# A transformer kernel whose weights pass in tiles of 2,048 columns instead of 1,024

## The chip, the core and the metric

The kernel runs on one core of a Trainium2 chip. The metric is the device time of one execution in microseconds. Before the change the median of three runs is 2656.81 us (2655.06 to 2656.96).

The engines that matter: TensorE (PE in the profile; PEld is its weight load) multiplies, VectorE (DVE) and ScalarE (ACT) work on elements, SyncE (SP) issues the loads. One issue is carried out by the core's 16 DMA engines together.

## The reference, cut to what matters

The input is 256 tokens of 1,024 features, in float32. Two blocks follow one another:

```
first block, 2 layers:  x = LN(a*x + hybrid_mixer(x));  x = LN(a*x + f(x))
    f: layer 0 a dense SwiGLU (2816 wide); layer 1 eight experts (3584 wide), 2 per token
second block, 2 layers: x = LN(a*x + swiglu/2); x = LN(a*x + attention(x))
                        x = LN(a*x + memory_attn(x, mem)); x = LN(a*x + swiglu/2)
swiglu(x, w_gate, w_up, w_down) = (silu(x @ w_gate) * (x @ w_up)) @ w_down
memory_attn: k, v = split(mem @ w_kv), 256 memory tokens, 4 heads of 256
```

The attention of layer 0 is a global one and a windowed one side by side ("ab"), that of layer 1 a neighbourhood one ("mc"). `hybrid_mixer` is a gated linear attention beside a spatial gating.

## The kernel before, in words

Nearly all time goes into matmuls against weights that are read once from memory, some 650 MB. Each float32 weight is split on the chip into a rounded part (hi) and a remainder (lo), each activation likewise, and each product is three matmuls (`mm3`: hi by hi, lo by hi, hi by lo, lines 207 to 209), with 512 columns of output.

`split_weight` (line 190) is the path of every weight tile of 128 x 1024: SyncE loads 512 KB into a `raw` tile (line 193), ScalarE casts it to `whi` (line 195), VectorE subtracts to get `wlo` (line 197). The three tiles come from rings of seven, nine and eight (`wraw`, `whi`, `wlo` in `body`), 4 KB per partition each, 96 KB together. A raw slot comes free when the subtraction has read it, a hi or lo slot when the last matmul on it is done; the load, cast or subtraction that needs the slot waits for that. A tile is 2 blocks of 128 rows by 512 columns where 512 outputs are made from all 1,024 features (`accumulate_k4`), or one block of 128 rows by 1,024 columns where 1,024 outputs are made (`accumulate_k2`); `units(c, w, u, n)` makes 2n of them.

The Python code is the order of issue only in outline: a scheduler places every instruction in its engine's queue when the program is built, and each engine then works through its queue in that order. So one long instruction in front of a short one on VectorE delays it, and the engines meet through semaphores.

The stages, in order: hybrid mixer, dense FFN, hybrid mixer, experts, FFN, ab, memory attention, FFN, FFN, mc, memory attention, FFN. In an FFN, five groups of gate and up columns (and one of half the width) and then three groups of down rows are each used by two blocks of 128 tokens. In the expert stage (`moe`) the tokens of one expert are gathered into 128 slots, so each tile is used by one pass: eight gate and up tiles, four down tiles per iteration, seven iterations per expert, 56 in all. Per iteration ScalarE computes silu, VectorE multiplies (line 770), TensorE transposes (line 304), the result is split (hTh, hTl, lines 295 and 296), and `down` of the iteration before runs. An expert's result is split (yh, yl) and scattered back with matmuls (lines 758 and 759) and an addition into X on VectorE (line 760); the gather of the next two experts (line 725) is spread over iterations.

The memory's keys and values do not depend on the tokens. They are eight `MemBlock`s, each with two tiles of memory rows and four of weights, two halves of 48 matmuls. Two are done at the start of the expert stage, one at its end (loaded ahead of the last down tiles, computed after them), three in ab, two in mc, filling gaps there.

Of the kernel before, what the change touches and what calls it, by code (L numbers as in the profile page):

```python
# [8 lines left out]
F32 = mybir.dt.float32  # L9
# [16 lines left out]
UW = 1024  # L26
# [65 lines left out]
def k4_units(w):  # L92
    n = w.shape[-1]
    b = w.reshape(4, 2, P, n // 512, 512).transpose(3, 0, 2, 1, 4)
    return np.ascontiguousarray(b).reshape(-1, P, UW)


def k2_units(w):
    return np.ascontiguousarray(w).reshape(-1, P, UW)

# [15 lines left out]
def layout(a):  # L116
# [5 lines left out]
    o["memT"] = feature_major(a["mem_2"].reshape(S, D))  # L122
# [20 lines left out]
    moe = np.empty((8, 7, 12, P, UW), np.float32)  # L143
    for i, n in enumerate(("exp_w_gate", "exp_w_up")):
        w = a[n][0].reshape(8, 4, 2, P, 7, 512).transpose(0, 4, 1, 3, 2, 5)
        moe[:, :, 4 * i:4 * i + 4] = w.reshape(8, 7, 4, P, UW)
    moe[:, :, 8:12] = a["exp_w_down"][0].reshape(8, 7, 4, P, UW)
    o["moe"] = moe.reshape(8 * 84, P, UW)
# [41 lines left out]
def split_weight(c, src):  # L190
    nc = c.nc
    raw = c.wraw.tile([P, UW], F32, name="raw")
    nc.sync.dma_start(raw, src)
    hi = c.whi.tile([P, UW], F32R, name="whi")
    nc.scalar.copy(hi, raw)  # L195
    lo = c.wlo.tile([P, UW], F32R, name="wlo")
    nc.vector.tensor_sub(lo, raw, hi.bitcast(F32))  # L197
    return hi, lo


def units(c, dram, u0, n):
    return [split_weight(c, dram[2 * u0 + i]) for i in range(2 * n)]
# [9 lines left out]
def accumulate_k4(c, ps, xk, us):  # L212
    for k in range(8):
        h, l = us[k // 2]
        sl = slice(512 * (k % 2), 512 * (k % 2) + 512)
        mm3(c, ps, *xk(k), h[:, sl], l[:, sl], k == 0, k == 7)


def accumulate_k2(c, pss, xk, us, k0, nk, half_major=False):
    order = [(i, half) for i in range(len(us)) for half in range(2)]  # L220
    if half_major:
        order.sort(key=lambda o: o[1])
    for i, half in order:
        h, l = us[i]
        k = k0 + i
        sl = slice(512 * half, 512 * half + 512)
        mm3(c, pss[half], *xk(k), h[:, sl], l[:, sl], k == 0, k == nk - 1)
# [19 lines left out]
class MemBlock:  # L247
# [3 lines left out]
    def load(self):  # L251
        c = self.c
        self.m = [split_weight(c, c.A["memT"][i]) for i in range(2)]
        self.us = units(c, c.A[f"m_kv{self.l}"], 4 * self.which + 2 * self.blk, 2)

    def at(self, k, sl):
        o = 256 * (k % 4)
        return [x[:, o + sl.start:o + sl.stop] for x in self.m[k // 4]]

    def half(self, half):  # L260
        c, nc = self.c, self.c.nc
        ps = c.acc.tile([P, 512], F32, name="acc")
        if self.which == 0:
            for f in (2 * half, 2 * half + 1):
                out = ps[:, 256 * (f % 2):256 * (f % 2) + 256]
                for k in range(8):
                    wh, wl = self.us[k // 2]
                    sl = slice(512 * (k % 2) + P * f, 512 * (k % 2) + P * f + P)
# [13 lines left out]
    def steps(self):  # L282
        def first():
            self.load()
            self.half(0)

        return [first, lambda: self.half(1)]
# [100 lines left out]
def project(c, w, u0, nblk, xT, epi, us=None):  # L388
    us = us or units(c, w, u0, 2 * nblk)
    for t in range(2):  # L390
        pss = []
        for b in range(nblk):
            ps = acc_tile(c)
            accumulate_k4(c, ps, tok(xT, t), us[4 * b:4 * b + 4])
            pss.append(ps)
        epi(t, pss)
# [16 lines left out]
def ffn(c, w, X, xT, ln_idx, halved, want_xT=True):  # L413
    nc = c.nc
    with c.tc.tile_pool(name="ffn", bufs=1) as fp:
# [3 lines left out]
        for j in range(6):  # L419
            us = units(c, w, 4 * j, 4 if j < 5 else 2)  # L420
            n = 512 if j < 5 else 256
            for t in range(2):
                g = acc_tile(c)
                accumulate_k4(c, g, tok(xT, t), us[:4])
# [3 lines left out]
                if j < 5:  # L428
                    u = acc_tile(c)
                    accumulate_k4(c, u, tok(xT, t), us[4:])  # L430
                else:
                    u = g[:, 256:]
# [8 lines left out]
        for u0, n in ((0, 3), (3, 4), (7, 4)):  # L441
            us = units(c, w, 22 + u0, n)
            for t in range(2):
                accumulate_k2(c, pss[t], tok((hh, hl), t), us, 2 * u0, 22, u0 == 7)
# [3 lines left out]
                if u0 == 7:  # L448
# [328 lines left out]
def moe(c, X, xT, ln_idx):  # L777
    nc, A = c.nc, c.A
    W = A["moe"]
    with c.tc.tile_pool(name="moeb", bufs=1) as c.big, c.tc.tile_pool(name="moe", bufs=1) as mp:  # L780
# [11 lines left out]
        def gu(e, j):  # L792
# [3 lines left out]
            for b in range(2):  # L796
                accumulate_k4(c, pss[b], slots_of(xg, e % 2), us[4 * b:4 * b + 4])
# [56 lines left out]
def crowded(c, mp, W, slot, gate, XS, Xn):  # L854
    nc, tc = c.nc, c.tc
    for e in range(N_EXP):
# [6 lines left out]
        with tc.For_i(0, 7, 1) as j:  # L863
            def halves(u):
                raw = c.lnp.tile([P, D], F32, name="lnb")
                nc.sync.dma_start(raw, W[bass.ds(j * 12 + (84 * e + u), 1), :, :].rearrange("a p n -> (a p) n"))
                for half in range(2):
                    sl = slice(512 * half, 512 * half + 512)
                    hi = mp.tile([P, 512], F32R, name="chi")
                    nc.scalar.copy(hi, raw[:, sl])  # L870
                    lo = mp.tile([P, 512], F32R, name="clo")
                    nc.vector.tensor_sub(lo, raw[:, sl], hi.bitcast(F32))
                    yield half, hi, lo

            pss = [acc_tile(c), acc_tile(c)]
            for b in range(2):
                for i in range(4):
                    for half, hi, lo in halves(4 * b + i):
                        k = 2 * i + half
# [3 lines left out]
            for k in range(4):  # L883
                for half, hi, lo in halves(8 + k):
# [128 lines left out]
def mixer_ab(c, X, xT, ln_idx):  # L1013
    nc, A = c.nc, c.A
    with c.tc.tile_pool(name="ab", bufs=1) as ap:
# [89 lines left out]
        for b in take(c, c.F[3]):  # L1105
            steps += b.steps()
# [4 lines left out]
def mixer_c(c, X, xT, ln_idx):  # L1111
    nc, A = c.nc, c.A
    with c.tc.tile_pool(name="mc", bufs=1) as ap:
# [58 lines left out]
        for b in take(c, c.F[4]):  # L1172
            steps += b.steps()
# [54 lines left out]
def body(tc, A, out, stages=STAGES):  # L1228
# [4 lines left out]
    with tc.tile_pool(name="const", bufs=1) as cp, \  # L1233
            tc.tile_pool(name="wraw", bufs=7) as c.wraw, tc.tile_pool(name="whi", bufs=9) as c.whi, \
            tc.tile_pool(name="wlo", bufs=8) as c.wlo, \
# [7 lines left out]
        c.early = []  # L1243
        for i in range(4):
            raw = c.wraw.tile([P, UW], F32, name="raw")
            nc.sync.dma_start(raw[:, 0:512], A["xT"][i // 2][:, 512 * (i % 2):512 * (i % 2) + 512])
            ks = slice(2 * i, 2 * i + 2)
            split(c, raw[:, 0:512].rearrange("p (k t s) -> p k t s", k=2, t=2), xT[0][:, ks], xT[1][:, ks])
            if stages[0].startswith("hyb"):
                c.early.append(split_weight(c, A[f"h_in{stages[0][3]}"][i]))  # L1250
# [42 lines left out]
```

## Time and profile before

| what | value |
|---|---|
| median of three runs | 2656.81 us |
| the profiled execution | 2656.44 us, its span 2654.6 us, mean granted clock 0.996 |
| TensorE busy | 2596.9 us, 98% of the span |
| VectorE busy | 1899.9 us, 72%; of this 1407.2 in 1193 subtractions (line 197) |
| ScalarE busy | 1483.8 us, 56%; of this 1194.0 in 1193 casts (line 195) |
| moved by DMA | 658.65 MB, mean 248 GB/s, 69.7% of the 16 engines' time |
| loads of expert weights | 672 of 512 KB |

The page's shares are means over twelve stages that differ: the expert stage takes from about 400 to 1490 us and moves over half of the bytes; FFN stages use each tile twice. A matmul's busy time overlaps its neighbours', so distances from start to start tell the pace. A row of the timeline gives start, duration, engine, line and operation, output and inputs, and in brackets the idle time before it with what ended it. Rows with xN are N such instructions in a run.

### The profile page before, as it was taken

What the parts mean: (1) busy time and instruction counts of PE and PEld (TensorE: products, weight loads), DVE (VectorE), ACT (ScalarE), POOL (GpSimd) and SP (SyncE); (2) the same over time, 40 slices, a digit from 0 to 9 for tenths busy, and PEclk for the clock granted to TensorE, in tenths of its full rate; (3) what the DMA queues carried; (4) which work ended last, traced back from release to release, by engine and by line L of the source; (5) the groups of instructions that cost most, each with busy time, mean ns of one, the idle gap of its engine ahead of it and who ended that gap; (6) DMA issues with size and microseconds to landing.
All of it is one profiled execution on the core that took longest, in us unless ns stands there. A gap on an engine that the chain in (4) does not pass through costs nothing. (4 is left out here: it accounts for less than half of the span.)

```text
span 2654.6 us, 34354 instructions
## 1 busy us (share of the span) xinstructions
PE 2596.9 (98%) x12226; PEld 2110.3 (79%) x12226; DVE 1899.9 (72%) x2306; ACT 1483.8 (56%) x1780; POOL 46.8 (2%) x57
## 2 busy tenths in 40 slices
PE   8999999999999999999999999999999999999998
PEld 6888778877777777787777788788888888788887
DVE  6754668888888888888888655866755656566664
ACT  5444447676777777767777444554443443544552
POOL 1000000000000000000000000100000000000000
PEclk9999999999999999999999999999999999999999
DMA  7555536999999999999999655544554655744562
GB/s 287 175 180 192 199 127 249 341 355 348 333 348 354 341 338 347 345 347 332 358 346 355 221 191 206 184 168 175 206 187 149 221 204 154 231 155 175 206 206 88
DMA packets 193980, 658.65 MB, mean 248 GB/s; under 512 B 33094, under 2 KB 33288, under 8 KB 193288
## 3 DMA queue, kind: packets, MB, share of 16 engines
q1 hardware_dynamic: 193800, 656.37, 69.7%
q8 instruction: 98, 1.61, 0.2%
q14 instruction: 82, 0.67, 0.1%
HBM read 651.05 MB, written 5.24 MB: 247 GB/s over the span
## 5 line engine op out<-in xcount | busy, mean ns | idle before, releaser
L197 DVE TENSOR_TENSOR wlo<-raw,whi 128x1024 fp32r<-128x1024 f32 x1193 | 1407.2, 1219 | 237.1 <-ACT whi L195 113.2
L195 ACT CAST whi<-raw 128x1024 fp32r<-128x1024 f32 x1193 | 1194.0, 1053 | 373.2 <-PE acc L209 291.0
L207 PE MATMUL acc<-whi,xh 128*128 128x512 f32 x1312 | 522.0, 398 | 6.6 <-ACT whi L195 6.3
L209 PE MATMUL acc<-whi,xl 128*128 128x512 f32 x1312 | 514.9, 393 | 0.0
L208 PE MATMUL acc<-wlo,xh 128*128 128x512 f32 x1312 | 514.1, 392 | 0.0
L208 PE MATMUL acc<-wlo,xgh 128*128 128x512 f32 x896 | 356.9, 398 | 5.3 <-DVE wlo L197 5.3
L207 PE MATMUL acc<-whi,xgh 128*128 128x512 f32 x896 | 350.2, 391 | 1.9 <-ACT whi L195 1.9
L209 PE MATMUL acc<-whi,xgl 128*128 128x512 f32 x896 | 350.3, 391 | 0.0
L207 PEld LDWEIGHTS acc<-whi,xh 128*128 128x128 f32 x1312 | 247.5, 189 | 56.5 <-ACT whi L195 6.3
L209 PEld LDWEIGHTS acc<-whi,xl 128*128 128x128 f32 x1312 | 247.0, 188 | 52.0 <-issue 0.5
L208 PEld LDWEIGHTS acc<-wlo,xh 128*128 128x128 f32 x1312 | 247.5, 189 | 50.1 <-DVE wlo L197 0.8
L208 PEld LDWEIGHTS acc<-wlo,xgh 128*128 128x128 f32 x896 | 168.0, 188 | 63.5 <-DVE wlo L197 27.8
L207 PEld LDWEIGHTS acc<-whi,xgh 128*128 128x128 f32 x896 | 168.2, 188 | 40.9 <-ACT whi L195 4.8
L209 PEld LDWEIGHTS acc<-whi,xgl 128*128 128x128 f32 x896 | 168.3, 188 | 32.6
L208 PE MATMUL tp<-wlo,hTh 128*128 128x512 f32 x448 | 180.1, 402 | 7.3 <-DVE wlo L197 7.1
L209 PE MATMUL tp<-whi,hTl 128*128 128x512 f32 x448 | 178.5, 398 | 0.0
L207 PE MATMUL acc<-whi,hh 128*128 128x512 f32 x440 | 172.5, 392 | 0.0
L209 PE MATMUL acc<-whi,hl 128*128 128x512 f32 x440 | 171.4, 390 | 0.0
L208 PE MATMUL acc<-wlo,hh 128*128 128x512 f32 x440 | 171.3, 389 | 0.0
L207 PE MATMUL tp<-whi,hTh 128*128 128x512 f32 x448 | 153.9, 394 | 5.0 <-ACT whi L195 5.0
L296 DVE TENSOR_TENSOR hl<-tp,hh 128x512 fp32r<-128x512 f32 (+1 forms) x60 | 38.8, 647 | 136.9 <-ACT hh L295 135.5
L295 ACT CAST xh<-tp 128x512 fp32r<-128x512 f32 x52 | 30.2, 588 | 172.9 <-PE tp L304 159.2
(254 smaller groups left out, 2490.2 us busy)
## 6 DMA issues: line engine op xcount, KB each, us to landing
raw<-moe_dram SPq DMA_DIRECT2D x672, 512.0 KB, 5.4
raw<-f_dram SPq DMA_DIRECT2D x330, 512.0 KB, 5.0
raw<-h_in_dram SPq DMA_DIRECT2D x40, 512.0 KB, 6.0
raw<-m_kv_dram SPq DMA_DIRECT2D x32, 512.0 KB, 4.5
raw<-c_in_dram SPq DMA_DIRECT2D x24, 512.0 KB, 5.3
raw<-h_out_dram SPq DMA_DIRECT2D x16, 512.0 KB, 4.4
raw<-memT_dram SPq DMA_DIRECT2D x16, 512.0 KB, 4.6
raw<-m_q_dram SPq DMA_DIRECT2D x16, 512.0 KB, 5.6
```

Source lines behind the costliest of these rows:

```text
L195: nc.scalar.copy(hi, raw)
L197: nc.vector.tensor_sub(lo, raw, hi.bitcast(F32))
L207: mm(ps, xh, wh, start=start, stop=False)
L208: mm(ps, xh, wl, start=False, stop=False)
L209: mm(ps, xl, wh, start=False, stop=stop)
L295: c.nc.scalar.copy(dh, ps)
L296: c.nc.vector.tensor_sub(dl, ps, dh.bitcast(F32))
```

## The change

A weight tile gets 2,048 columns: one load of 1 MB, one cast, one subtraction. The rings become four, four and four tiles of 8 KB per partition, again 96 KB. A k4 tile now holds four blocks of rows by 512 columns, a k2 tile two blocks by 1,024. `units` makes n tiles where it made 2n. The three groups of an FFN's down rows become four, four and three tiles (8, 8, 6 blocks of rows) where they were 6, 8 and 8 blocks, so the last group is shorter. The memory rows become one tile of 1 MB, and in ab and mc a block takes over the rows of the block ahead of it instead of loading them again (`block_steps`): 5 loads of 1 MB in place of 16 of 512 KB in all. The first mixer's first two tiles are loaded, cast and subtracted in halves, and the input's transposed copy shares one raw tile. The matmuls are the same and as many, and stand in nearly the same order. (`crowded`, which the inputs do not reach, is adapted alike; its part of the diff is left out, as is the host's reshaping.)

```diff
-UW = 1024
+UW = 2048
...
-def split_weight(c, src):
+def split_weight(c, src, parts=1):
     nc = c.nc
+    n = src.shape[-1]
     raw = c.wraw.tile([P, UW], F32, name="raw")
-    nc.sync.dma_start(raw, src)
     hi = c.whi.tile([P, UW], F32R, name="whi")
-    nc.scalar.copy(hi, raw)
     lo = c.wlo.tile([P, UW], F32R, name="wlo")
-    nc.vector.tensor_sub(lo, raw, hi.bitcast(F32))
+    for i in range(parts):
+        sl = slice(n // parts * i, n // parts * (i + 1))
+        nc.sync.dma_start(raw[:, sl], src[:, sl])
+        nc.scalar.copy(hi[:, sl], raw[:, sl])
+        nc.vector.tensor_sub(lo[:, sl], raw[:, sl], hi[:, sl].bitcast(F32))
     return hi, lo
 
 
 def units(c, dram, u0, n):
-    return [split_weight(c, dram[2 * u0 + i]) for i in range(2 * n)]
+    return [split_weight(c, dram[u0 + i]) for i in range(n)]
...
-    def load(self):
+    def load(self, m=None):
         c = self.c
-        self.m = [split_weight(c, c.A["memT"][i]) for i in range(2)]
+        self.m = m or split_weight(c, c.A["memT"])
...
+def block_steps(blocks):
+    def step(i, half):
+        if half == 0:
+            blocks[i].load(blocks[i - 1].m if i else None)
+        blocks[i].half(half)
+
+    return [lambda i=i, half=half: step(i, half) for i in range(len(blocks)) for half in range(2)]
...
-        for u0, n in ((0, 3), (3, 4), (7, 4)):
+        for u0, n in ((0, 4), (4, 4), (8, 3)):
...
-            tc.tile_pool(name="wraw", bufs=7) as c.wraw, tc.tile_pool(name="whi", bufs=9) as c.whi, \
-            tc.tile_pool(name="wlo", bufs=8) as c.wlo, \
+            tc.tile_pool(name="wraw", bufs=4) as c.wraw, tc.tile_pool(name="whi", bufs=4) as c.whi, \
+            tc.tile_pool(name="wlo", bufs=4) as c.wlo, \
...
+        raw = c.wraw.tile([P, UW], F32, name="raw")
         for i in range(4):
-            raw = c.wraw.tile([P, UW], F32, name="raw")
-            nc.sync.dma_start(raw[:, 0:512], A["xT"][i // 2][:, 512 * (i % 2):512 * (i % 2) + 512])
+            sl = slice(512 * i, 512 * i + 512)
+            nc.sync.dma_start(raw[:, sl], A["xT"][i // 2][:, 512 * (i % 2):512 * (i % 2) + 512])
...
-                c.early.append(split_weight(c, A[f"h_in{stages[0][3]}"][i]))
+            if i % 2 == 0 and stages[0].startswith("hyb"):
+                c.early.append(split_weight(c, A[f"h_in{stages[0][3]}"][i // 2], 2))
```

VectorE's queue in an iteration of the expert loop with a scatter, before (wlo is a weight's remainder; silu the multiply of line 770; X the scatter's addition; hTl the remainder of the transposed product):

```order
L197 TENSOR_TENSOR wlo<-raw,whi 128x1024 x10
L770 TENSOR_TENSOR silu<-silu,acc 128x512
L197 TENSOR_TENSOR wlo<-raw,whi 128x1024
L760 SCALAR_TENSOR_TENSOR X<-tp,gate,X 128x512
L296 TENSOR_TENSOR hTl<-tp,hTh 128x512
L197 TENSOR_TENSOR wlo<-raw,whi 128x1024 x11
```

The same place after the change:

```order
L776 TENSOR_TENSOR silu<-silu,acc 128x512
L201 TENSOR_TENSOR wlo<-raw,whi 128x2048
L302 TENSOR_TENSOR hTl<-tp,hTh 128x512
L766 SCALAR_TENSOR_TENSOR X<-tp,gate,X 128x512
L201 TENSOR_TENSOR wlo<-raw,whi 128x2048 x5
L776 TENSOR_TENSOR silu<-silu,acc 128x512
```

Six instructions stand in an iteration where twelve stood, and X and hTl have changed places. Behind the multiply comes the second of two down tiles, where before it was the second of four.

VectorE's queue between the first FFN and the second mixer, before, from the second token block's residual sum (line 343) to the layer norm's last step (line 359):

```order
L344 BN_STATS lst<-X 128x6
L197 TENSOR_TENSOR wlo<-raw,whi 128x1024
L353 BN_AGGR lmv<-lst 128x2
L197 TENSOR_TENSOR wlo<-raw,whi 128x1024
L327 TENSOR_SCALAR lrs<-lmv 128x1
L358 SCALAR_TENSOR_TENSOR X<-X,lmv,lng 128x512 x2
L359 SCALAR_TENSOR_TENSOR X<-X,lrs,lnb 128x512 x2
```

The same place after the change:

```order
L350 BN_STATS lst<-X 128x6
L201 TENSOR_TENSOR wlo<-raw,whi 128x2048
L359 BN_AGGR lmv<-lst 128x2
L201 TENSOR_TENSOR wlo<-raw,whi 128x2048
L333 TENSOR_SCALAR lrs<-lmv 128x1
L364 SCALAR_TENSOR_TENSOR X<-X,lmv,lng 128x512 x2
L365 SCALAR_TENSOR_TENSOR X<-X,lrs,lnb 128x512 x2
```

Two subtractions stand inside the layer norm in both; each has twice the columns after the change.

SyncE's queue of loads at the end of the expert stage, before (moe are the experts' tiles, memT and m_kv those of the extra memory block, f_00 the next FFN's):

```order
L193 DMA raw<-moe_dram 128x1024 x657
L193 DMA raw<-memT_dram 128x1024 x2
L193 DMA raw<-m_kv_dram 128x1024 x4
L193 DMA raw<-moe_dram 128x1024 x4
L193 DMA raw<-f_00_dram 128x1024 x7
```

The same place after the change:

```order
L199 DMA raw<-moe_dram 128x2048 x329
L199 DMA raw<-memT_dram 128x2048
L199 DMA raw<-m_kv_dram 128x2048 x2
L199 DMA raw<-moe_dram 128x2048 x2
L199 DMA raw<-f_00_dram 128x2048 x4
```

The memory block's tiles still go ahead of the last down tiles; they are three where they were six, in a ring of four where the rings had seven to nine.

## Rows read from the trace of the kernel before

**Rows 1.** The page: busy time, share of the span, instructions.

```profile
PE 2596.9 (98%) x12226; PEld 2110.3 (79%) x12226; DVE 1899.9 (72%) x2306; ACT 1483.8 (56%) x1780; POOL 46.8 (2%) x57
```

**Rows 2.** Windows (FFN, expert loop, two experts): length, busy by engine, clock, DMA share, GB/s.

```profile
1526.00:1592.40 66.40, 66.40 (x306) 54.95 (x305) 35.64 (x36) 30.57 (x36) 0.00 (x0) 1.00 0.55 191
455.00:1450.00 995.00, 975.30 (x4336) 775.75 (x4335) 857.85 (x825) 708.16 (x795) 0.00 (x0) 1.00 0.95 347
1100.00:1356.50 256.50, 250.84 (x1118) 199.46 (x1117) 221.15 (x212) 182.55 (x206) 0.00 (x0) 1.00 0.95 344
```

**Rows 3.** Groups by line and shape: count, busy us, mean ns, idle before.

```profile
L197 DVE TENSOR_TENSOR wlo<-raw,whi 128x1024 fp32r<-128x1024 f32 x1193 | 1407.2, 1219 | 237.1 <-ACT whi L195 113.2 <-PE acc L208 85.6 <-PE acc L209 9.9
L195 ACT CAST whi<-raw 128x1024 fp32r<-128x1024 f32 x1193 | 1194.0, 1053 | 373.2 <-PE acc L209 291.0 <-DMA raw<-moe_dram 30.1 <-PE acc L208 7.0
...
L296 DVE TENSOR_TENSOR hTl<-tp,hTh 128x512 fp32r<-128x512 f32 x56 | 38.2, 682 | 0.0
...
L295 ACT CAST hTh<-tp 128x512 fp32r<-128x512 f32 x56 | 32.9, 587 | 104.1 <-PE tp L304 104.0
```

**Rows 4.** Timeline, expert loop: TensorE, then VectorE; start, us, instruction, idle before.

```profile
735.87 0.62 PE L207 MATMUL tp<-whi,hTh 128*128 128x512 f32 x2
...
737.01 0.60 PE L304 MATMUL tp<-cst,silu 128*128 128x128 f32 x4
...
737.91 0.40 PE L209 MATMUL tp<-whi,hTl 128*128 128x512 f32 x1
...
739.53 0.61 PE L207 MATMUL tp<-whi,hTh 128*128 128x512 f32 x2
740.64 0.50 PE L208 MATMUL tp<-wlo,hTh 128*128 128x512 f32 x1 [0.50 <-DVE wlo L197]
...
736.07 0.69 DVE L770 TENSOR_TENSOR silu<-silu,acc 128x512 f32<-128x512 f32 x1 [0.66 <-PE acc L209]
736.67 1.22 DVE L197 TENSOR_TENSOR wlo<-raw,whi 128x1024 fp32r<-128x1024 f32 x1
738.11 0.75 DVE L760 SCALAR_TENSOR_TENSOR X<-tp,gate,X 128x512 f32<-128x512 f32 x1 [0.22 <-PE tp L759]
738.78 0.68 DVE L296 TENSOR_TENSOR hTl<-tp,hTh 128x512 fp32r<-128x512 f32 x1
739.37 3.49 DVE L197 TENSOR_TENSOR wlo<-raw,whi 128x1024 fp32r<-128x1024 f32 x3
```

**Rows 5.** Timeline, TensorE, two other iterations of the loop.

```profile
707.61 0.50 PE L208 MATMUL acc<-wlo,xgh 128*128 128x512 f32 x1 [0.76 <-DVE wlo L197]
...
718.28 0.66 PE L304 MATMUL tp<-cst,silu 128*128 128x128 f32 x4 [0.78 <-DVE silu L770]
```

**Rows 6.** Waits in the expert loop: us in total, times, longest.

```profile
ACT whi L195 <- DMA raw<-moe_dram: 28.2, 36, 1.8
...
PE tp L208 <- DVE wlo L197: 6.6, 13, 0.5
```

**Rows 7.** Waits of the load queue, 600 to 1300 us.

```profile
SPq L193 <- DVE wlo L197: 506.4, 452, 2.9
```

**Rows 8.** DMA: 512 KB expert loads (page); two 1 MB loads (tile kT).

```profile
raw<-moe_dram SPq DMA_DIRECT2D x672, 512.0 KB, 5.4
...
DMA to landing us min/median/max: 7.7/7.8/7.8
```

**Rows 9.** Timeline, TensorE: start and end of the expert stage.

```profile
408.74 0.39 PE L209 MATMUL acc<-whi,wlo 128*128 128x256 f32 x1 [0.50 <-DVE wlo L197]
...
1457.93 0.80 PE L207 MATMUL tp<-whi,hTh 128*128 128x512 f32 x1 [4.99 <-ACT whi L195]
```

**Rows 10.** Timeline, first FFN to second mixer: VectorE, then TensorE.

```profile
301.07 1.21 DVE L197 TENSOR_TENSOR wlo<-raw,whi 128x1024 fp32r<-128x1024 f32 x1
...
302.31 1.17 DVE L197 TENSOR_TENSOR wlo<-raw,whi 128x1024 fp32r<-128x1024 f32 x1
...
307.63 0.63 PE L304 MATMUL tp<-cst,X 128*128 128x128 f32 x4 [3.15 <-DVE X L359]
```

More of the change, by code (lines that the diff above doesn't have):

```diff
@@ L213, in accumulate_k4 @@
     for k in range(8):
-        h, l = us[k // 2]
-        sl = slice(512 * (k % 2), 512 * (k % 2) + 512)
+        h, l = us[k // 4]
+        sl = slice(512 * (k % 4), 512 * (k % 4) + 512)
         mm3(c, ps, *xk(k), h[:, sl], l[:, sl], k == 0, k == 7)
 def accumulate_k2(c, pss, xk, us, k0, nk, half_major=False):
-    order = [(i, half) for i in range(len(us)) for half in range(2)]
+    order = [(i, half) for i in range(2 * len(us)) for half in range(2)]
     if half_major:
@@ L223, in accumulate_k2 @@
     for i, half in order:
-        h, l = us[i]
+        h, l = us[i // 2]
         k = k0 + i
-        sl = slice(512 * half, 512 * half + 512)
+        o = D * (i % 2) + 512 * half
+        sl = slice(o, o + 512)
         mm3(c, pss[half], *xk(k), h[:, sl], l[:, sl], k == 0, k == nk - 1)
@@ L447, in ffn @@
                 late = []
-                if u0 == 7:
+                if u0 == 8:
                     xn, st = residual(c, X[t], pss[t], ALPHA * (2.0 if halved else 1.0))
@@ L863, in crowded, with quarters @@
         with tc.For_i(0, 7, 1) as j:
[L864 to L873, printed above, removed]
+            def quarters(u):
+                for i in range(2):
+                    raw = c.lnp.tile([P, D], F32, name="lnb")
+                    src = W[bass.ds(j * 6 + (42 * e + u), 1), :, :].rearrange("a p n -> (a p) n")
+                    nc.sync.dma_start(raw, src[:, D * i:D * i + D])
+                    for half in range(2):
+                        sl = slice(512 * half, 512 * half + 512)
+                        hi = mp.tile([P, 512], F32R, name="chi")
+                        nc.scalar.copy(hi, raw[:, sl])
+                        lo = mp.tile([P, 512], F32R, name="clo")
+                        nc.vector.tensor_sub(lo, raw[:, sl], hi.bitcast(F32))
+                        yield i, half, hi, lo
             pss = [acc_tile(c), acc_tile(c)]
             for b in range(2):
-                for i in range(4):
-                    for half, hi, lo in halves(4 * b + i):
-                        k = 2 * i + half
+                for u in range(2):
+                    for i, half, hi, lo in quarters(2 * b + u):
+                        k = 4 * u + 2 * i + half
                         mm3(c, pss[b], *slots_of(xg, 0)(k), hi, lo, k == 0, k == 7)
@@ L882, in crowded @@
             pss = [acc_tile(c), acc_tile(c)]
-            for k in range(4):
-                for half, hi, lo in halves(8 + k):
+            for u in range(2):
+                for i, half, hi, lo in quarters(4 + u):
+                    k = 2 * u + i
                     mm3(c, pss[half], hT[0][:, k], hT[1][:, k], hi, lo, k == 0, k == 3)
@@ L1104, in mixer_ab @@
         steps = late_steps(c, xT, A["ab_in"], 4, lambda t, ps: q_epi(t, ps, 1))
-        for b in take(c, c.F[3]):
-            steps += b.steps()
+        steps += block_steps(take(c, c.F[3]))
         attend(pair, 8, {i: [f] for i, f in enumerate(steps)})
@@ L1171, in mixer_c @@
             steps += late_steps(c, xT, W, 6 + 2 * n, lambda t, ps, f=f: f(t, ps, 1))
-        for b in take(c, c.F[4]):
-            steps += b.steps()
+        steps += block_steps(take(c, c.F[4]))
         plan = {0: steps[0:2], 1: steps[2:4], 2: steps[4:5], 3: steps[5:6]}
```

42 lines of the change are left out of this document (18 added, 24 removed).

## The prediction, made before the changed kernel had run

> **What bounds the kernel now.** The page's busy line comes first: TensorE 98% of the span, VectorE 72%, ScalarE 56% [rows 1]. An average like that hides stages, so the windows view is next. In an FFN (1526 to 1592.4 us) TensorE is busy for the whole window, with VectorE at 35.6 of 66.4 us and the DMA engines at a share of 0.55 [rows 2]; there is nothing to win there, only something to lose. In the expert loop (455 to 1450 us) TensorE is busy 975.3 of 995 us, VectorE 858, and the DMA share is 0.95 at 347 GB/s [rows 2]. So the loop, a third of the time, is where weights are late: 19.7 us of listed idle. A listed stall of 0.50 us costs more than it shows, since the pipeline restarts: two matmuls start at 739.53 and 739.76, the next would start at 739.99 and starts at 740.64, and its successor another 0.11 us late, 0.76 us in all [rows 4]. By that ratio (1.5) the loop's idle is worth about 30 us, and that is the most that the change can win there.
>
> Who is late? In the waits view the load queue is held by VectorE's subtraction 452 times, 506 us over 700 us [rows 7]: the loads run as fast as raw slots come free. ScalarE waits for data in only 36 cases, 28 us, and TensorE for a lo part in 13 cases, 6.6 us [rows 6]. So the loop is limited by the order of VectorE's queue more than by the transfers, but the transfers are not far behind.
>
> **Term 1: FFN stages, 0.** A tile of 2,048 columns feeds 12 matmuls per token block. A gate/up group is four tiles, all of the ring, read by both token blocks. A slot comes free in the second pass after its 12 matmuls, and three more tiles' work (36 matmuls at 0.23 us, 8.3 us) covers its successor. That needs a cast and a subtraction. Their durations at 2,048 columns are estimates from the shapes at hand [rows 3]: the subtraction takes 682 ns for 512 columns and 1,219 for 1,024, so 537 more per 512 and 2.29 us at 2,048 (two old ones take 2.44); the cast goes 587, 1,053, so about 1.98 us (two old ones 2.11). Together 4.3 us, with 4 us left for the silu, the multiply and the splits that stand in the two queues. Cover gone, an FFN group would lose what exceeds 8.3 us; I see none. From both sides: 0 to +3 us over five FFNs.
>
> **Term 2: the expert loop, -8.8 us.** Per iteration it uses 12 tiles before, 6 after. The timeline shows the stall that repeats [rows 4]. VectorE's queue is multiply (736.07), lo of the second down tile (736.67), the scatter's addition X (738.11), hTl (738.78), and only then lo of the third down tile (739.37), which TensorE wants at 739.99. After the change one down tile holds what two held, and VectorE's order is multiply, lo of the last down tile, hTl, X, next gate tile. The last down tile is thus prepared ahead of X and hTl. In steps: 736.07 + 0.60 (multiply) = 736.67; a step of 2.21 (the three subtractions from 739.37 take 3.49, so a step at 1,024 is 1.135 and at 2,048 about 1.135 + 2 x 0.537 = 2.21) gives 738.88; hTl 0.59 and X 0.67 give 740.14; another 2.21 gives 742.35 for the next gate tile's lo. TensorE gets there at 735.87 + 24 x 0.231 (seven steps from 737.91 to 739.53 in 1.62 us) + 0.90 (transposes and the scatter's first pair, 737.01 to 737.91) = 742.31. So it loses about 0.1 plus the restart's 0.11, 0.2 in place of 0.76: 0.55 us won. The waits view has 13 of these [rows 6]; a window of two experts shows four, and a few records are missing, so I count 16: 8.8 us.
>
> The other two kinds stay. Where the results of an expert are split (0.76 us at 707.61), the two half splits still alternate with subtractions; where TensorE's transposes follow directly on the up pass (0.78 us at 718.28) they wait for the multiply, which does not change [rows 5]. Bounds: all 30 us won; or the coarse ring costs up to the first rival's +28.
>
> **Term 3: start and end of the expert stage, +4.5 us.** At the start the ring of four holds the router's tile, the memory rows and two weight tiles, so the second memory block cannot start loading until the first has been used; before, seven raw and nine hi slots let it in. Today's small stall there is 0.50 us listed [rows 9]. I take one more cast and subtraction at 1,024 columns (1.05 + 1.22) and one such stall with its restart (0.76), +3 us; bounds 0 and +6. At the end, TensorE waits 4.99 us for the hi part of the last down tiles [rows 9], while the extra memory block sits in the ring. It then holds three of four slots, and the two last down tiles go one after the other through the fourth: the second's cast and subtraction (4.3 us) are bare, where before they lay beside matmuls, but the first one's casts are fewer. I take +1.5 us, bounds 0 and +4.3.
>
> **Term 4: from one stage to the next, +2.7 us.** At the first FFN's end the mixer needs both token blocks. VectorE has two subtractions of 1,024 columns inside the second layer norm (301.07 and 302.31), and TensorE waits 3.15 us for X until 307.63 [rows 10]. The order after keeps two there, of 2,048: 2 x (2.29 - 1.22) = +2.1 us. Elsewhere the first token block's pass hides such delays; for the mixers' chains and the attention I add +1 (bounds -1 and +5: each weight instruction in front of a chain step is a microsecond longer, but there are half as many). Shared memory rows remove three 1 MB loads with their casts and subtractions, but in stages where VectorE and ScalarE have room: -0.4 (bounds -2 and 0).
>
> **Sum.** -8.8 + 0 + 4.5 + 2.7 = -1.6. The profiled execution took 2656.44 us (span 2654.6), so 2654.8; the median of the runs is 0.4 above it. I forecast 2655 us: a small gain in the loop that the stage edges nearly eat.
>
> **Rivals.** *The ring of four becomes the limit (slower).* A raw slot's round is the load, cast and subtraction. A single 1 MB load today lands 7.8 us after issue, among other traffic [rows 8]; with 1.98 + 2.29 that is 12.1 us for four tiles, 18.1 us per iteration of six. The iteration today takes 256.5/14 = 18.3 [rows 2]. So the ring decides as soon as a load takes over 7.9 us from issue to landing. One microsecond over that adds 1.5 us to each iteration, 84 us over 56; a third of that, an average landing of 8.2 us, gives +28: 2683 us. For it: the DMA share is 0.95 already, and a slot returns in lumps of 1 MB. Against: with one slot free at a time, a load seldom queues behind a full one, and today's 512 KB land in 5.4 us while queued [rows 8].
>
> *Edges only.* The loop's stall just moves to the next gate tile (my margin there was 0.04 us), and the edges cost their upper half: +6 +4 +2 +3 = 15, so 2671; with the taken values, 2663. For it: every edge in terms 3 and 4 has a bare wait today. Against: the loop's order does move the late subtraction forward.
>
> *The loop fills.* Six fewer loads, casts and subtractions per iteration (VectorE saves 6 x 0.06 = 0.4 us by the steps of term 2, 6 x 0.15 = 0.9 by the means [rows 3]) let VectorE and the transfers run ahead; then 30 us go, less the edges' 7: 2633. For it: VectorE is at 86% in the loop, and stalls come from it. Against: the share of 0.95 leaves 5% of 995 us, and two of the three stalls are order, not load.
>
> The Trainium skill ("DMA: Bandwidth & Descriptors", Rules for kernel authors) asks for at least 1 MiB per DMA for full bandwidth, which would put this change on the side of the third rival. By that rule the loop's 512 KB loads should run below the rate; the trace has the engines at a share of 0.95 with them, several in flight, so it does not bear the rule out here, and the rival's chance rests on VectorE.
>
> **Numbers.** My forecast case, 2644 to 2662, has 0.42; the ring 0.20, edges 0.16, the loop that fills 0.22. A difference under 0.2%, 5.3 us, cannot be told from none here. Of the forecast case 0.17 is faster than 2651.5, 0.21 within, 0.04 slower; of the edges' 0.06 within, 0.10 slower; the ring is slower, the filled loop faster. That makes 0.39 faster, 0.27 the same, 0.34 slower. The range takes in the third rival and the ring's +28: 2632 to 2684.
>
> **What the changed profile would show.** Right: listed stalls before down tiles' lo parts gone, iterations with a scatter near 17.8 us, FFN windows still full, larger single waits at the expert stage's ends and before the second mixer. The ring as the limit: ScalarE's casts waiting for expert loads in most iterations, TensorE waiting for hi. The third rival: TensorE busy over 990 of the loop's 995 us with the loop some 30 us shorter. I am wrong if the FFN windows show gaps, or if a 1 MB expert load takes more than 8 us to land.

## The result, and the profile after

The changed kernel takes 2676.79 us (median of five, 2668.61 to 2677.23) against 2656.06 before: a ratio of 1.0069 (95% interval 1.0054 to 1.0084), 20.7 us slower. I had forecast 2655 and a chance of 0.34 for slower. The profiled execution took 2672.5 us, its span 2670.7, 16.1 over the span before; what the profile can place is thus 16.1 of the 20.7 us.

The page's lines of the changed kernel, as in [rows 1, 3, 8]:

```profile
PE 2594.6 (97%) x12226; PEld 2116.7 (79%) x12226; DVE 1840.3 (69%) x1710; ACT 1416.4 (53%) x1184; POOL 45.8 (2%) x57
...
L201 DVE TENSOR_TENSOR wlo<-raw,whi 128x2048 fp32r<-128x2048 f32 (+1 forms) x597 | 1349.7, 2277 | 452.5 <-ACT whi L200 451.6
L200 ACT CAST whi<-raw 128x2048 fp32r<-128x2048 f32 (+1 forms) x597 | 1126.0, 1903 | 500.9 <-PE acc L213 345.2
...
raw<-moe_dram SPq DMA_DIRECT2D x336, 1024.0 KB, 6.7
```

VectorE and ScalarE are busy 60 and 67 us less, as fewer and longer instructions should make it (2,290 and 1,913 ns a whole tile; the estimates were 2,293 and 1,985). But the subtraction's idle time that ended with the cast went from 113 us [rows 3] to 452: VectorE now often stands still until a cast is done. The windows view, an FFN and the expert loop, as in [rows 2]:

```profile
1534.00:1600.40 66.40, 66.40 (x306) 54.94 (x306) 34.44 (x24) 29.13 (x24) 0.00 (x0) 1.00 0.51 190
455.00:1450.00 995.00, 972.12 (x4360) 785.58 (x4360) 846.62 (x501) 695.10 (x472) 0.00 (x0) 1.00 0.94 349
```

The FFN is full, as before. To see where the time went I cut both traces at ScalarE's silu instructions (124 in either) and took the differences of the stretches between them:

| stretch | before, us | change, us | what the prediction had |
|---|---|---|---|
| first mixer, to the FFN's second silu | 129.40 | +1.8 | in term 4 |
| first FFN | 108.14 | 0.0 | 0 |
| to the second mixer's last silu | 146.87 | +0.8 | +2.1 and part of +1 |
| to the first silu of the experts | 67.13 | +4.7 | in +3 |
| the first two iterations | 26.48 | +3.7 | in +3 |
| the rest of the expert loop | 963.28 | -9.7 | -8.8 |
| its end, to the next FFN's third silu | 76.83 | +6.6 | +1.5 |
| FFN | 96.76 | 0.0 | 0 |
| ab, first memory attention | 274.45 | +5.6 | part of +1, less 0.4 |
| two FFNs | 295.10 | +0.2 | 0 |
| mc, second memory attention | 294.10 | +2.0 | part of +1 |
| last FFN and end | 176.12 | +0.3 | 0 |

So every edge but the one to the second mixer costs more than predicted, 25.8 us in all with the FFNs' remainder, and the loop gives back 9.7.

The loop's iteration with a scatter, TensorE and then VectorE, the changed kernel's answer to [rows 4]:

```profile
752.79 0.39 PE L211 MATMUL acc<-whi,xgh 128*128 128x512 f32 x1
753.02 0.49 PE L212 MATMUL acc<-wlo,xgh 128*128 128x512 f32 x1
753.35 0.40 PE L213 MATMUL acc<-whi,xgl 128*128 128x512 f32 x1
...
746.61 0.69 DVE L776 TENSOR_TENSOR silu<-silu,acc 128x512 f32<-128x512 f32 x1 [0.72 <-PE acc L213]
747.22 2.29 DVE L201 TENSOR_TENSOR wlo<-raw,whi 128x2048 fp32r<-128x2048 f32 x1
749.42 0.69 DVE L302 TENSOR_TENSOR hTl<-tp,hTh 128x512 fp32r<-128x512 f32 x1
750.02 0.74 DVE L766 SCALAR_TENSOR_TENSOR X<-tp,gate,X 128x512 f32<-128x512 f32 x1
750.68 4.48 DVE L201 TENSOR_TENSOR wlo<-raw,whi 128x2048 fp32r<-128x2048 f32 x2
```

The order is the one predicted: multiply, last down tile, hTl, X, next gate tile. From the multiply to the end of the next gate tile's subtraction, the first of the last two, is 746.61 to 752.92 (half of 4.48 us after 750.68), 6.31 us for the 6.28 of term 2, and TensorE has no listed wait: its lo product starts on time at 753.02, the next one 0.10 us late. In the waits view over the loop the waits for a down tile's lo part (`tp`) fell from 13 cases and 6.6 us [rows 6] to 6 and 2.6. But those for a gate or up tile's lo part (`acc`) rose; before, then after:

```profile
PE acc L208 <- DVE wlo L197: 5.3, 7, 0.8
...
PE acc L207 <- ACT whi L195: 1.9, 7, 0.3
```

```profile
ACT whi L200 <- DMA raw<-moe_dram: 105.7, 125, 2.6
...
PE acc L212 <- DVE wlo L201: 12.2, 30, 0.8
...
PE tp L212 <- DVE wlo L201: 2.6, 6, 0.9
```

Of these 30 waits 23 stand at the first lo product of the gate tile behind the down tiles: the stall has in part moved there, as the second rival had it. The iteration shown is one of those without it. To see the sum I added up what each step from one 128x512 matmul to the next takes beyond 0.227 us, over the loop of the table's row: at lo parts of down tiles 14.0 us before and 6.6 after, at lo parts of gate and up tiles 20.7 and 23.7, at hi parts 7.0 and 2.8.

The first line of the second view is the first rival's sign: casts wait for loads 125 times, where it was 36 [rows 6]. But a load lands 6.7 us after issue in the median (at most 8.7 in the loop), under the 7.9 from which the ring would decide, the waits for hi parts are gone from the view, and the loop is shorter. The ring did not take over.

The start and the end of the expert stage on TensorE, as in [rows 9]; the first line is from the kernel before:

```profile
412.20 0.39 PE L209 MATMUL acc<-whi,wlo 128*128 128x256 f32 x1 [1.77 <-DVE wlo L197]
...
411.51 0.50 PE L211 MATMUL acc<-whi 128*128 128x256 f32 x2 [1.09 <-ACT whi L200]
...
416.57 0.58 PE L213 MATMUL acc<-whi,wlo 128*128 128x256 f32 x1 [4.02 <-DVE wlo L201]
...
1460.75 1.22 PE L211 MATMUL tp<-whi,hTh 128*128 128x512 f32 x2 [6.07 <-ACT whi L200]
1463.08 0.80 PE L212 MATMUL tp<-wlo,hTh 128*128 128x512 f32 x1 [1.10 <-DVE wlo L201]
1463.67 0.63 PE L213 MATMUL tp<-whi,hTl 128*128 128x512 f32 x1
1464.10 0.63 PE L212 MATMUL tp<-wlo,hTh 128*128 128x512 f32 x1
...
1469.70 1.22 PE L211 MATMUL tp<-whi,hTh 128*128 128x512 f32 x2 [1.99 <-ACT whi L200]
1472.03 0.80 PE L212 MATMUL tp<-wlo,hTh 128*128 128x512 f32 x1 [1.11 <-DVE wlo L201]
```

At the start waits of 1.09 and 4.02 us stand where 0.50 and 1.77 stood; the second of these, 3.5 us behind the one in [rows 9], I had not seen. At the end the wait for the first down tile is 6.07 us for 4.99, and then come three more, 1.10, 1.99 and 1.11. The matmuls between them start 0.43 us apart (1463.67 to 1464.10): that is TensorE at the lower of its two clock levels (1.2 for 2.4 GHz) after the long wait; the windows view gives a granted clock of 0.50 from 1460 to 1475.

From the first FFN to the second mixer: ScalarE, VectorE, TensorE.

```profile
298.17 5.51 ACT L200 CAST whi<-raw 128x2048 fp32r<-128x2048 f32 x3 [0.79 <-PE acc L213]
...
300.12 2.29 DVE L201 TENSOR_TENSOR wlo<-raw,whi 128x2048 fp32r<-128x2048 f32 x1 [1.56 <-ACT whi L200]
...
302.46 0.50 PE L212 MATMUL acc<-wlo,xh 128*128 128x512 f32 x1 [1.38 <-DVE wlo L201]
...
307.28 0.50 PE L212 MATMUL acc<-wlo,xh 128*128 128x512 f32 x1 [1.78 <-DVE wlo L201]
```

Before, TensorE's one listed wait at this edge was for X [rows 10]. Now it waits twice for the lo part of a tile whose hi part it has begun to use: the cast starts at 298.17, the subtraction only at 300.12 when the whole cast is done, and TensorE goes on at 302.46. These waits lie where TensorE before waited for X, so little is lost by them here: X comes 2.3 us later than before (311.69 for 307.63, less the first mixer's 1.8), term 4 had 2.1, and at the second mixer's last silu 0.8 us are left. In ab a short step is caught behind a cast of 1.89 us; the wait before, then ScalarE and TensorE after:

```profile
1701.41 0.70 PE L955 MATMUL acc<-kT,qT 64*128 64x256 f32 x4 [0.79 <-ACT kT L1077]
...
1710.58 1.89 ACT L200 CAST whi<-raw 128x2048 fp32r<-128x2048 f32 x1
1712.37 0.59 ACT L1086 COPY kT<-tp 128x512 f32<-128x512 f32 x1
...
1713.01 0.70 PE L964 MATMUL acc<-kT,qT 64*128 64x256 f32 x4 [2.31 <-ACT kT L1086]
```

### The profile page after: what moved, and what is told of

Same layout as the page of the kernel before. It is cut to its first block, busy times and chain, and to the rows that moved or that the text cites. A ratio compares the mean times of both kernels' runs of the same rounds, so it can differ in the third digit from the quotient of the medians.

```text
span 2670.7 us, 30301 instructions
## 1 busy us (share of the span) xinstructions
PE 2594.6 (97%) x12226; PEld 2116.7 (79%) x12226; DVE 1840.3 (69%) x1710; ACT 1416.4 (53%) x1184; POOL 45.8 (2%) x57
## 5 line engine op out<-in xcount | busy, mean ns | idle before, releaser
L201 DVE TENSOR_TENSOR wlo<-raw,whi 128x2048 fp32r<-128x2048 f32 (+1 forms) x597 | 1349.7, 2277 | 452.5 <-ACT whi L200 451.6
L200 ACT CAST whi<-raw 128x2048 fp32r<-128x2048 f32 (+1 forms) x597 | 1126.0, 1903 | 500.9 <-PE acc L213 345.2
L211 PE MATMUL tp<-whi,hTh 128*128 128x512 f32 x448 | 166.7, 397 | 8.1 <-ACT whi L200 8.1
L301 ACT CAST xh<-tp 128x512 fp32r<-128x512 f32 x52 | 29.6, 589 | 186.0 <-PE tp L310 167.3
L212 PEld LDWEIGHTS tp<-wlo,hTh 128*128 128x128 f32 x448 | 85.6, 191 | 30.0 <-DVE wlo L201 12.0
```

The lines of the kernel that those rows point to most:

```text
L200: nc.scalar.copy(hi[:, sl], raw[:, sl])
L201: nc.vector.tensor_sub(lo[:, sl], raw[:, sl], hi[:, sl].bitcast(F32))
L211: mm(ps, xh, wh, start=start, stop=False)
L212: mm(ps, xh, wl, start=False, stop=False)
L301: c.nc.scalar.copy(dh, ps)
```

## The experiments

Edits are to the changed kernel unless another is named. The table gives medians of the timed runs, the ratio to the kernel before with its interval, and the stretches of the profiled execution, in us against before (edges: the first mixer, the way to the experts, their first two iterations, ab and mc together). Every stretch is from one execution. The loop of the changed kernel, of that with the extra block behind and of the filler is the same instructions in the same order and came out at -9.7, -5.8 and -7.3, their ab at +5.6, +5.5 and +7.1; so much is scatter.

| kernel | median | ratio | edges | loop | expert end |
|---|---|---|---|---|---|
| changed kernel | 2676.79 | 1.0069 (1.0054-1.0084) | +18.6 | -9.7 | +6.6 |
| extra block behind | 2665.72 | 1.0041 (1.0027-1.0055) | +16.5 | -5.8 | -3.9 |
| cast and subtraction in halves | 2654.64 | 0.9999 (0.9989-1.0008) | +2.2 | -5.3 | +1.9 |
| own slots | 2650.85 | 0.9981 (0.9972-0.9991) | -1.9 | -6.1 | -0.4 |
| 512 KB loads | 2653.94 | 0.9995 (0.9985-1.0004) | -1.7 | -0.9 | -0.6 |
| filler | 2675.59 | 1.0079 (1.0062-1.0096) | +20.2 | -7.3 | +3.3 |
| before, extra block behind | 2651.14 | 0.9983 (0.9973-0.9993) | -0.1 | -0.9 | -4.2 |
| own slots, extra block behind | 2645.78 | 0.9964 (0.9950-0.9978) | -1.3 | -5.8 | -4.9 |
| wide in the loop alone | 2647.71 | 0.9969 (0.9957-0.9982) | +5.2 | -8.2 | -6.4 |
| cast alone in halves | 2682.57 | 1.0102 (1.0085-1.0119) | +17.3 | +3.2 | +5.1 |
| subtraction alone in halves | 2706.61 | 1.0195 (1.0178-1.0212) | +13.1 | +33.9 | +2.4 |
| own slots, block behind, no sharing | 2647.49 | 0.9971 (0.9958-0.9983) | +1.8 | -4.5 | -5.6 |

**The extra memory block behind the last down tiles.**

```diff
         extra = take(c, c.F[2])
-        for b in extra:
-            b.load()
         pe, pj, phT, y = pend
         down(pe, pj, phT, y)
+        for b in extra:
+            b.load()
```

> The changed kernel, with the extra memory block loaded behind the last two down tiles of the expert stage instead of ahead of them. Theory (slots): at the end of the expert stage the block's three tiles hold three of the four slots, so the last down tile's cast waits until TensorE is done with the one before (two waits of 2.4 and 1.5 us, most of it at half clock, where before there is none). With the down tiles first both have a slot: these two waits go, the half-clock stretch is shorter, and the stage's end takes 4 to 7 us less; time 3 to 7 us below the changed kernel. Rival (width): the waits come from the length of one cast and one subtraction, the order of loads does not matter, within 1.5 us of the changed kernel, or later since the block's own tiles come later.

Measured: 11 us below the changed kernel, and the stage's end 10.5 us shorter, of which the loop takes back 3.9; as its instructions are the same, I read nothing into that. The waits for down tiles are gone. The slots theory holds for this place, and its price was larger than I had put it.

**Cast and subtraction in halves.**

```diff
-        nc.scalar.copy(hi[:, sl], raw[:, sl])
-        nc.vector.tensor_sub(lo[:, sl], raw[:, sl], hi[:, sl].bitcast(F32))
+    for i in range(n // 1024):
+        sl = slice(1024 * i, 1024 * (i + 1))
+        nc.scalar.copy(hi[:, sl], raw[:, sl])
+        nc.vector.tensor_sub(lo[:, sl], raw[:, sl], hi[:, sl].bitcast(F32))
```

> The changed kernel (1 MB loads, rings of four slots of 2,048 columns) with each tile cast and subtracted in two halves of 1,024 columns. Theory (width of one instruction): at the stage edges a 2.0 us cast and a 2.3 us subtraction stand in front of short steps and of the first matmul; in halves the edges outside the expert stage's end lose 10 of their 19 us, and the expert loop loses its 10 us gain (the scatter's addition again comes ahead of a down tile's half): 2672 to 2678 in all, edges smaller, loop longer. Rival (slots): the edges keep their cost, loop loses its gain: 2682 to 2690. Rival (loads): as the slots.

Measured: 22 us below the changed kernel, and the same as before the change. The edges fall from +18.6 to +2.2 with loads and slots as they were: the expectation had the direction right and was 17 us too timid, and the rivals of slots and loads fall as the main cause of the edges. By stretch: first mixer +1.8 to +1.6, second mixer +0.8 to -3.6, start of the experts with two iterations +8.4 to +3.5, ab +5.6 to +1.2, mc +2.0 to -0.6. The same place as above, ScalarE, VectorE, TensorE:

```profile
297.96 5.79 ACT L202 CAST whi<-raw 128x1024 fp32r<-128x1024 f32 x6 [0.81 <-PE acc L215]
...
299.05 2.36 DVE L203 TENSOR_TENSOR wlo<-raw,whi 128x1024 fp32r<-128x1024 f32 x2 [0.71 <-ACT whi L202]
...
304.29 0.50 PE L214 MATMUL acc<-wlo,xh 128*128 128x512 f32 x1 [0.70 <-DVE wlo L203]
```

The first subtraction starts 1.09 us after the first cast (1.95 in the changed kernel); of the two waits the first is gone and the second is 0.70 us in place of 1.78, with one of 0.40 behind it.

**Which half of the pair?** The cast alone in halves, then the subtraction alone:

```diff
+    for i in range(n // 1024):          # the cast alone
+        sl = slice(1024 * i, 1024 * (i + 1))
+        nc.scalar.copy(hi[:, sl], raw[:, sl])
+    nc.vector.tensor_sub(lo[:, :n], raw[:, :n], hi[:, :n].bitcast(F32))
...
+    nc.scalar.copy(hi[:, :n], raw[:, :n])          # the subtraction alone
+    for i in range(n // 1024):
+        sl = slice(1024 * i, 1024 * (i + 1))
+        nc.vector.tensor_sub(lo[:, sl], raw[:, sl], hi[:, sl].bitcast(F32))
```

> The changed kernel with the cast in two halves and the subtraction whole. If the wide cast on ScalarE is what costs at the edges (a kT or a silu that waits behind 1.9 us), the edges come near those of the kernel with both in halves, 2657 to 2662. If the wide subtraction on VectorE costs (the first lo part comes 2.3 us after hi, and layer-norm steps wait behind it), little changes, 2668 to 2676.

> The changed kernel with the subtraction in two halves and the cast whole. If the subtraction is what costs at the edges: 2656 to 2662, with the stalls between a hi product and the lo product behind it at about half. If the cast costs: 2668 to 2676.

Both expectations were wrong: each alone is slower than the changed kernel, by 6 and by 30 us. That lies in the loop; the edges cost 1.3 and 5.5 us less, where both together take off 16.4. So neither instruction's length alone accounts for the edges. The cast alone in halves, at the same place:

```profile
298.39 5.79 ACT L202 CAST whi<-raw 128x1024 fp32r<-128x1024 f32 x6 [0.81 <-PE acc L215]
...
300.42 2.29 DVE L203 TENSOR_TENSOR wlo<-raw,whi 128x2048 fp32r<-128x2048 f32 x1 [1.66 <-ACT whi L202]
...
302.76 0.50 PE L214 MATMUL acc<-wlo,xh 128*128 128x512 f32 x1 [1.46 <-DVE wlo L203]
...
307.54 0.50 PE L214 MATMUL acc<-wlo,xh 128*128 128x512 f32 x1 [1.74 <-DVE wlo L203]
```

And the subtraction alone:

```profile
299.50 5.52 ACT L200 CAST whi<-raw 128x2048 fp32r<-128x2048 f32 x3 [0.85 <-PE acc L215]
...
301.44 1.23 DVE L203 TENSOR_TENSOR wlo<-raw,whi 128x1024 fp32r<-128x1024 f32 x1 [1.61 <-ACT whi L200]
...
305.55 0.50 PE L214 MATMUL acc<-wlo,xh 128*128 128x512 f32 x1 [1.17 <-DVE wlo L203]
```

With the cast in halves the whole subtraction still waits for both, 2.03 us after the first began, and TensorE waits as in the changed kernel (1.46 and 1.74). With the subtraction in halves it still waits for the whole cast (1.94 us), though its first half then comes early enough for the first wait to fall to 0.35 us: to the second mixer this kernel is at -3.0, nearly as with both in halves, but ab and mc keep their cost (+5.3 and +1.9; +7.6 and +2.2 with the cast alone). Only both together overlap: the second cast runs beside the first subtraction. The edges follow the chain of one tile, from the start of its cast to its first lo columns: 1.95 + 2.29 = 4.2 us when both are whole (edges +18.6), 2.03 + 2.29 = 4.3 with the cast in halves (+17.3), 1.94 + 1.23 = 3.2 with the subtraction (+13.1), 1.09 + 1.23 = 2.3 with both (+2.2). What each place owes to this chain, and what to short steps behind a long instruction, is not separated.

The 34 us in the loop of the last kernel are another matter, the order of ScalarE's queue:

```profile
745.23 0.60 ACT L777 ACTIVATE silu<-acc 128x512 f32<-128x512 f32 x1 [3.52 <-PE acc L215]
745.72 5.51 ACT L200 CAST whi<-raw 128x2048 fp32r<-128x2048 f32 x3
...
748.94 0.50 PE L214 MATMUL acc<-wlo,xgh 128*128 128x512 f32 x1 [0.77 <-DVE wlo L203]
```

Here three casts stand between silu and hTh in 42 of 53 iterations, where the changed kernel has two in all; ScalarE waits for TensorE in front of the silu, and the cast behind it comes too late. Of 38.9 us of listed waits for gate and up lo parts 29.6 are of this one kind, 39 waits of 0.76 us about 3.7 us after a silu. Casts wait for loads no longer than in the changed kernel (92.8 us, 105.7).

**Slots of their own, then 512 KB loads.**

```diff
+    for i in range(n // 1024):
+        sl = slice(1024 * i, 1024 * (i + 1))
+        hi = c.whi.tile([P, 1024], F32R, name="whi")          # 8 slots
+        nc.scalar.copy(hi, raw[:, sl])
+        lo = c.wlo.tile([P, 1024], F32R, name="wlo")          # 8 slots
+        nc.vector.tensor_sub(lo, raw[:, sl], hi.bitcast(F32))
```

> As the kernel with halves, but each half of hi and lo has a slot of its own (eight and eight of 1,024 columns); the loads stay 1 MB in a ring of four. Theory (width): little more is won than by halving the instructions, 0 to 3 us. Rival (slots): here the edges and the expert stage's end come back to the time before, 15 to 20 us less than with whole slots, 2658 to 2664. Rival (loads): the edges still cost 10 us or more, above 2666.

```diff
+        raw = c.wraw.tile([P, 1024], F32, name="raw")          # in the loop above, 8 slots
+        nc.sync.dma_start(raw, src[:, sl])
```

> As the kernel with own slots, but the loads too are of 512 KB, in eight slots of 1,024 columns: the granularity of the kernel before, with rings of 8, 8 and 8 for 7, 9 and 8, shared memory rows and the FFN's new groups of down rows. Theories of width and of slots: no more than 2 us from the kernel with own slots. Rival (loads of 1 MB land late): this step alone brings the time back, 8 us or more. What is left against the kernel before is the sharing, the groups and the rings: within 3 us of it if these are worth nothing.

Measured: own slots win 3.8 us over halves in whole slots, and 512 KB loads lose 3.1 of it. So slots that come back in lumps cost a few microseconds, most of them at the start of the experts (+3.5 to +0.4 with two iterations) and in the first mixer (+1.6 to +0.3), and loads of 1 MB are worth about three in all; in the loop of the two traces 5.2 (-6.1 against -0.9), half of that in late steps at hi parts (3.7 us against 6.2). To the second mixer these two kernels and the one with halves are 3.1 to 3.6 us faster than before; whether the new groups of down rows or the rings do that, no run separates. Their windows over 455 to 1450 us, the 1 MB loads first, then the 512 KB:

```profile
455.00:1450.00 995.00, 973.06 (x4333) 775.75 (x4331) 865.13 (x829) 716.74 (x799) 0.00 (x0) 1.00 0.93 349
```

```profile
455.00:1450.00 995.00, 975.25 (x4336) 775.95 (x4334) 859.50 (x826) 704.56 (x797) 0.00 (x0) 1.00 0.95 347
```

The 1 MB loads moved a little more with a share of 0.93 for 0.95. The rule that I had weighed asks for at least 1 MiB per DMA for full bandwidth (the Trainium skill, "DMA: Bandwidth & Descriptors", Rules for kernel authors). This pair leans to its side, by about 2% of the engines' time where they are nearly full.

**A filler for TensorE**, 26 matmuls nobody reads, in the wait of 6 us:

```diff
+        z = tp_tile(c)
+        for i in range(26):
+            nc.tensor.matmul(z, phT[0][:, i % 4], XS[0][0][:, 0:512], start=True, stop=True)
         down(pe, pj, phT, y)
```

> The changed kernel with 26 matmuls of 128x512 whose result nobody reads, queued on TensorE ahead of the last two down tiles, where it waits 6.2 us (26 x 0.23 = 5.9 us of work). Theory (clock): about a third to a half of the cost of the expert stage's end is not the waiting but the matmuls behind it, which run at the lower of the two clock levels (0.43 us from start to start for 0.23); with TensorE kept at work the first down tile's 12 matmuls run at 0.23 and the stage's end takes 2.3 to 5 us less. Rival (waiting only): the clock falls anyway at the next two waits (2.4 and 1.5 us) or does not matter: within 1 us of the changed kernel there.

Measured: the stage's end 3.3 us shorter, as the clock theory had it; the time as a whole is the same within its spread (2675.59; ab came out 1.4 and the loop 2.4 us longer in the profiled execution). TensorE behind the filler:

```profile
1456.77 6.06 PE L845 MATMUL tp<-Xh,hTh 128*128 128x512 f32 x26
...
1464.64 0.50 PE L212 MATMUL tp<-wlo,hTh 128*128 128x512 f32 x1 [1.36 <-DVE wlo L201]
1464.97 0.40 PE L213 MATMUL tp<-whi,hTl 128*128 128x512 f32 x1
1465.21 0.40 PE L212 MATMUL tp<-wlo,hTh 128*128 128x512 f32 x1
```

The first down tile's matmuls now start 0.24 us apart (1464.97, 1465.21), though TensorE had waited 1.36 us before. The second tile is at the lower level as ever (granted clock 0.50 from 1470 to 1475 us). So the clock on the first tile is 3.3 of the 6.6 us that this place costs over before.

**The same edit in the kernel before, and the versions that beat both.** The first is the edit of the extra block made in the kernel before, the second the same edit on top of own slots; the third has the edit of the extra block and this one:

```diff
+    w = UW if c.wide else 1024          # c.wide: iterations 1 to 54 of the experts
+    for i in range(max(n // w, 1)):
+        sl = slice(w * i, min(w * (i + 1), n))
+        nc.scalar.copy(hi[:, sl], raw[:, sl])
+        nc.vector.tensor_sub(lo[:, sl], raw[:, sl], hi[:, sl].bitcast(F32))
```

> The kernel before with one edit: the extra memory block of the expert stage loaded behind the last down tiles. Theory (what the block's tiles do is hold up the down tiles, in either kernel): TensorE's wait of 5 us there shrinks to 1 or less, and with it the half-clock stretch of 9 us; 4 to 9 us less than before, 2647 to 2652. Rival (only the ring of four is hurt by it): within 2 us of before.

> The kernel with 1 MB loads and own slots for each half of hi and lo, with the extra memory block loaded behind the last down tiles. If the two gains lie in different places they add: 2651 less 3 to 8, 2643 to 2648, faster than the kernel before by 0.3% or more. If the own slots already took the wait away at the end of the expert stage: 2650 to 2652.

> The changed kernel with casts and subtractions of 2,048 columns only inside the expert loop (iterations 1 to 54 of 56) and halves of 1,024 everywhere else, and the extra memory block loaded behind the last down tiles. Theory (the wide instruction pays in the loop, where VectorE's order improves, and costs at the edges): the loop keeps 6 to 10 us of gain, the edges cost no more than 4: 2641 to 2648. Rival (wide instructions gain nothing in the loop, the 1 MB loads do): no better than the kernel with own slots and the same tail, 2646 or more.

The block's tiles hold up the down tiles in the kernel before too: 4.3 us are won, as expected. TensorE's remaining wait is the one for the branch that can lead to `crowded`, 7.49 us for 3.71, since the block's products now start behind it; before, then with the edit:

```profile
1475.26 0.47 PE L207 MATMUL acc<-whi 128*128 128x512 f32 x1 [3.71 <-DVEq L843]
...
1468.74 0.76 PE L207 MATMUL acc<-whi 128*128 128x512 f32 x1 [7.49 <-DVEq L843]
```

With own slots the two gains add: 2645.78 us, 9.7 below the kernel before in the same runs, the fastest here. Wide instructions in the loop alone keep -8.2 there, within the range of the changed kernel's loop (-5.8 to -9.7), but the experts' start costs +3.4 and the first two iterations +4.0: 2647.71, whose interval overlaps.

**No sharing of memory rows** in ab and mc, on the fastest kernel:

```diff
-            blocks[i].load(blocks[i - 1].m if i else None)
+            blocks[i].load()
```

> The fastest kernel so far (1 MB loads, own slots for halves, extra block behind the last down tiles) with memory blocks in ab and mc that load their own rows, 3 loads of 1 MB more. In the prediction's account sharing saves 0 to 2 us there, so this would be 0 to 2 us slower (2646 to 2648). Rival: rows that are kept hold two of eight slots through three blocks, and this is what still costs ab about 1 us in every kernel that shares: 1 us faster.

Measured: 1.7 us slower, intervals overlapping, with ab 2.8 us longer in the trace. So sharing is at most a small gain, and nothing shows that what ab still costs comes from it.

## Why the prediction was wrong, point by point

- Term 1 (FFN, 0) was right: 0.0 in single FFNs, 0.2 over two, and the window is full.
- Term 2 (loop, -8.8) came out at -9.7, and the scatter's stall went as worked out (14.0 to 6.6 us of late steps). But the agreement of the sum is luck, and the loop's own scatter is 4 us. The step that failed is the price of the next gate tile, "0.2 in place of 0.76": the stall in part moved there (20.7 to 23.7 us), as the second rival said. And waits for hi parts fell by 4.2 us, which I had not looked for. In the kernels of 1,024-column instructions the wait for the down tile stayed (13 cases, 6.5 us with halves), so their -5 to -6 comes from the 1 MB loads.
- Term 3 (+4.5) measured +15.0 (4.7 + 3.7 at the start, 6.6 at the end), the largest error. At the start the step that failed is "I take one more cast and subtraction at 1,024 columns (1.05 + 1.22) and one such stall with its restart (0.76), +3 us": it took the old durations, and only the first of two waits that were there. The runs put +8.4 in its place, of which halves take 4.9 and own slots 3.1 more. At the end I saw that the fourth slot alone was left, and that a cast and a subtraction would be bare; the step that failed there is "but the first one's casts are fewer. I take +1.5 us", which set those 4.3 us off against a gain that did not come, and left out that the matmuls behind the long wait run at the lower clock level (3.3 us by the filler). My own upper bound was 4.3.
- Term 4 (+2.7) measured +10.2 (1.8 + 0.8 + 5.6 + 2.0). The +2.1 for X was right where it was taken, but most of it was made up within the second mixer. The step that failed is "Elsewhere the first token block's pass hides such delays; for the mixers' chains and the attention I add +1 (bounds -1 and +5...)": the first mixer, ab and mc cost 9.4. I had counted what a wide instruction delays in the queues, +1.07 us here and there, and not that the weight's own preparation grows from 1.05 + 1.22 to 1.91 + 2.29 us in series. In an FFN 8.3 us of other matmuls cover that, which I worked out; at an edge I didn't ask. The experiment with halves takes 11.6 us off these four stretches with nothing else changed; the first mixer's 1.8 goes only with own slots.
- Rivals: "edges only" had the place right, and the stall that moves to the next gate tile in part, but at 2663 to 2671 and 0.16; it had no loop gain and still fell 6 us short. The ring as the limit was rejected by 6.7 us to land, and its time of 2683 is 6 us off on the other side, by another road. Of its signs the casts' waits for loads were seen (125 for 36); TensorE's waits for hi in the loop were not, they went from 7 to none.
- What stays open: the changed kernel's runs spread over 8.6 us, those before over 1.9, and the median is 4.3 us above the execution that was read. The fastest has the highest mean granted clock (a span of 2666.8 us at 0.995) and a slow one the lowest (2675.0 at 0.992), but three at 0.993 lie between 2670.7 and 2675.4. So the clock can tell only a part; no run here shows where the slow ones lose.

## What to carry to other kernels

Price a larger tile by its whole chain, from landing to the last derived part, and hold it against the work that covers it at every stage edge, not only in the steady loop; a chain of two engines over one tile should be cut so that the second starts on the first half. Large loads and small compute instructions can be had together: one DMA of 1 MB, halves behind it. And ask of each tile that is loaded early for later use which slot it takes from a tile that is needed now. A change of shapes can also reorder a queue: read every engine's order again, not VectorE's alone.

## What the runs showed of the hardware that was not expected

After a wait of 6.07 us TensorE's 128x512 matmuls started 0.43 us apart, and with work of no use in that wait 0.23 to 0.24, after a remaining wait of 1.36 us. Halving only one of two instructions in a chain cost 6 and 30 us, where halving both won 22; the 30 lie in the expert loop, in a queue whose order had changed with the shapes.
